# A two-layer hybrid block on one core: the recurrence as three streams in a TensorE order written by the program, and attention scores over the full array

## The chip, the cores and the metric

The kernel runs on one core of one Trainium2 chip. The metric is the device time of one execution, in microseconds; smaller is better. TensorE does the matrix products, VectorE (DVE), ScalarE (ACT) and GpSimd (POOL) the element-wise work, SyncE (SP) issues most transfers. Each engine executes its own list of instructions strictly in the order in which they stand in the built program.

## What is computed

Two layers act on 512 latent tokens and 256 context tokens of width 2048. Each layer normalises and modulates its input, multiplies it with one wide matrix (7872 columns), and feeds four groups of heads: a spatial-gating MLP, differential attention, a recurrence in two directions, and a short convolution. Each group is gated, the four are joined, and one output product follows. The change touches the recurrence, the attention scores and the convolution:

```python
def rwkv_scan(r, k, v, decay, kk, a, s0):
    def step(S, inp):
        r_t, k_t, v_t, w_t, kk_t, a_t = inp
        sa = jnp.einsum('bhvk,bhk->bhv', S, -kk_t)
        S = (S * w_t[:, :, None, :] + sa[..., None] * (kk_t * a_t)[:, :, None, :]
             + v_t[..., None] * k_t[:, :, None, :])
        y = jnp.einsum('bhvk,bhk->bhv', S, r_t)
        return S, y
...
def diff_attn_core(q, k, v, lam):
    s = _f32(jnp.einsum('bqhmd,bkhmd->bhmqk', q, k)) * (HD_QK ** -0.5)
    p = jax.nn.softmax(s, axis=-1)
    a = p[:, :, 0] - lam * p[:, :, 1]
```

## The kernel before

**Main passes.** Every column tile of the wide product (`mtile`, `mstep`) is computed transposed: 128 output columns by 512 latent tokens in one PSUM bank and by 256 context tokens in another. Weights and activations are each split into a high and a low part, and three products are summed (high by high, high by low, low by high), over 16 blocks of 128 rows. So a tile is 48 passes of 512 columns and, where the context is needed, 48 of 256. They all stand on line 306 and are called main passes here. The split of the weights (lines 276 and 277) is done by ACT and by POOL or DVE.

**The recurrence.** The 768 tokens are cut into three segments of 256 and each segment into four chunks of 64. Per layer there are four feature tiles by three segments by two directions: 24 segment rounds. A round has these parts:

- `seg_pre` and `seg_scores` prepare a segment. On TensorE: `lw`, `la` (lines 603 to 605), the squared norm `n` (line 684, called from line 631), the bonus sum `bs` (line 684, called from line 665), a transposition `vp`, the scores `g` (line 706) and a transposition `bt`. From `n` to `bs` there is a long way over other engines: square root on ACT (632), maximum, reciprocal and product on DVE (633, 634, 636), the products `bk` on POOL (652, 656), `BK` on DVE (658), the product `t_L` on DVE (661) and on POOL (663), and its split `hi`, `lo` (276, 277). `t_L` is written in place of a tile that `BK` reads, so line 661 stands behind line 658.
- `seg_inverse` inverts a triangular matrix by doubling: some 14 groups of products in f16 and fp32 (lines 804, 809, 848), each of which needs the group before it, after a copy on ACT or a product on DVE.
- `seg_chain` carries the state through four chunks: per chunk three products in a row, lines 745, 748 and 753, each after a copy or an update on DVE and ACT.
- `seg_y` makes the output, and after both directions of a feature tile `rwkv_merge` normalises it (lines 870 and 876).

`rwkv_pipe` emits these parts in rounds: the chain of segment n, the inverse of n+1, the preparation of n+2. Main passes of the projections are emitted between rounds. The final order on every engine, TensorE too, is made by the framework's scheduler, which moves main passes in between the products.

**Attention.** Per head and per block of 128 queries, `attention` computes the scores with a product over 128 rows (line 997, query high and low parts stacked by key high part) and a second one over 64 rows only (line 999, query high part by key low part `klo`), each over 256 and 512 keys.

Of the kernel before, what the change touches and what calls it, by code (L numbers as in the profile page):

```python
# [9 lines left out]
F32 = mybir.dt.float32  # L10
# [50 lines left out]

def shape_constants():
# [38 lines left out]
    return c, h, cs, rot  # L101


class Kernel:
# [188 lines left out]
    def mstep(self, grp, w, raw, q, first, last):  # L293

        nc = self.nc
# [12 lines left out]

    def mtile(self, w_ap, w, ctx, lat, q0=0, acc=None, pre=None):
        grp = self.mopen(w, ctx, lat, acc)  # L310
        for iq in range(4):
            q = (q0 + iq) % 4
            raw = pre[iq] if pre and iq < len(pre) else self.wload(w_ap, w, q)
            self.mstep(grp, w, raw, q, iq == 0, iq == 3)
# [5 lines left out]
    def proj(self, l, c0, ctx=True, acc=None):  # L320
        ahead = self.ahead.pop(c0, None)
        if ahead:
            if ctx and ahead[1][0] is None:
                return self.mtile(self.w_cols(l, c0), W_TILE_AT[c0], self.hc, None)[0], ahead[0][0]
            return ahead[1][0], ahead[0][0]
        return self.mtile(self.w_cols(l, c0), W_TILE_AT[c0], self.hc if ctx else None, self.hl, 0, acc)
# [104 lines left out]
    def recurrence(self, l):  # L431
        nc, tc, ps = self.nc, self.tc, self.ps
        need = l < DEPTH - 1
        with tc.tile_pool(name=self.nm("rw"), bufs=1, reuse_waits="tile") as rp:
# [12 lines left out]
            def gate_tiles(fts):  # L447
                for ft in fts:
                    p = self.proj(l, 5312 + ft * 128, ctx=need)
                    t = self.gate2(rp, p, "stg", 2)  # L450
                    lo = 0 if need else NCTX
                    nc.sync.dma_start(out=self.gd[ft][:, lo:T], in_=t[:, lo:T])

            def rkv_tile(ft, i, acc=None):
                p = self.proj(l, 3584 + i * 512 + ft * 128, ctx=(need or i > 0), acc=acc)
# [5 lines left out]
            if not need:  # L461
                gate_tiles(range(3))
                for ft in range(2):
                    rkv_tile(ft, 0, ((ps, "ps", 2), (ps, "ps", 2)))
                gate_tiles((3,))
                for ft in range(2, 4):
                    rkv_tile(ft, 0)
            for d in range(2):
# [3 lines left out]
                self.evac(raw[0:96, 2:258], raw[0:96, 260:772], self.proj(l, 5120 + 96 * d), 96)  # L472
# [16 lines left out]
            late = []  # L489
            for ft in range(4):  # L490
                for i in range(0 if need or ft >= 4 else 1, 3):
                    if ft:
                        late.append((6 * ft - 2 - 1, rkv_tile, (ft, i)))
                    else:
                        rkv_tile(ft, i)
                if need or ft >= 4:
                    late.append((6 * ft + 6 - 4, gate_tiles, ((ft,),)))
            late.sort(key=lambda x: x[0])
            for n in self.rwkv_pipe(l):
                while late and late[0][0] <= n + 1:  # L500
                    _, fn, args = late.pop(0)
                    fn(*args)
            for f in range((2, 4)[l]):
                self.conv(l, f)

    def rwkv_pipe(self, l):
# [7 lines left out]
        merge = None  # L514
        for n in range(-2, N + 1):
            gens = []
            if 0 <= n < N:
                gens.append((self.seg_chain(segs[n]), 5))
            if 0 <= n + 1 < N:
                gens.append((self.seg_inverse(segs[n + 1]), 8))  # L520
            if n + 2 < N:
                gens.append((self.seg_pre(segs[n + 2]), 4))
            if merge is not None:
                gens.append((merge, 3))
                merge = None
            prog = [0.0] * len(gens)
            live = set(range(len(gens)))
            while live:
                g = min(live, key=lambda x: (prog[x], x))
                try:  # L530
                    next(gens[g][0])
                    prog[g] += 1.0 / gens[g][1]
                except StopIteration:
                    live.discard(g)
            if 0 <= n < N:
                self.seg_y(segs[n])
                if segs[n]["last"]:
                    merge = self.rwkv_merge(l, segs[n]["ft"], segs[n]["st"]["yacc"], segs[n]["st"]["bacc"])
            if n + 2 < N:
                self.seg_scores(segs[n + 2])  # L540
            yield n

    def seg_pre(self, s):
# [55 lines left out]
        yield  # L599

        lw = ps.tile([128, 512], F32, tag="ps", name=self.nm("lw"))
        la = ps.tile([128, 512], F32, tag="ps", name=self.nm("la"))
        nc.tensor.matmul(out=lw[:, 0:SEG], lhsT=wh[:, 0, d, :], rhs=lz[:, 0, :], start=True, stop=False)
        nc.tensor.matmul(out=lw[:, 0:SEG], lhsT=wlo[:, d, :], rhs=lz[:, 0, :], start=False, stop=True)
        nc.tensor.matmul(out=la[:, 0:SEG], lhsT=wh[0:96, 1, d, :], rhs=lz[0:96, 1, :], start=True, stop=True)
        tw, ta = tmp("tw"), tmp("ta")
        A.activation(out=tw, in_=lw[:, 0:SEG], func=AF.Tanh, scale=0.5, bias=col(der["w0"], q))
        A.activation(out=ta, in_=la[:, 0:SEG], func=AF.Tanh, scale=0.5, bias=col(der["a0"], q))
# [20 lines left out]
        A.activation(out=sq, in_=z["k"], func=AF.Square, scale=col(der["kk"], q))  # L629
        n2 = ps.tile([128, 512], F32, tag="ps", name=self.nm("n2"))  # L630
# [6 lines left out]
        yield  # L637
# [21 lines left out]
        if want_y:  # L659
# [3 lines left out]
            G.tensor_tensor(out=rk, in0=rk, in1=ta, op=ALU.mult)  # L663
            bs = ps.tile([128, 512], F32, tag="ps", name=self.nm("bs"))
# [21 lines left out]
    def seg_scores(self, s):  # L686
        l, d, want_y, AR, BK, zv = (s[k] for k in ("l", "d", "want_y", "AR", "BK", "zv"))
        nc, rp, ps = self.nc, self.rp, self.ps
        V, G, A = nc.vector, nc.gpsimd, nc.scalar
        vp = ps.tile([128, 4, 128], F32, tag="ps", name=self.nm("vp"))  # L690
# [12 lines left out]
        for c2 in range(0, 4, 2):  # L703
            g = ps.tile([128, 2, 2, nk, 64], F32, tag="ps", name=self.nm("g"))
            for c in range(2):
                nc.tensor.matmul(out=g[:, c], lhsT=bkc(c2 + c), rhs=AR[:, c2 + c, :, 0:nk, :], start=True, stop=True)  # L706
            for c in range(2):
                mk = self.gmask[:, d:d + 1, 0:nk].to_broadcast([128, 2, nk, 64])
                V.tensor_tensor(out=GM[:, c2 + c, 0:nk].rearrange("p k h t -> p h k t"), in0=g[:, c], in1=mk,
                                op=ALU.mult)  # L710
        bt = ps.tile([128, 4, 128], F32, tag="ps", name=self.nm("bt"))
# [4 lines left out]
    def seg_chain(self, s):  # L716
# [5 lines left out]
        hs2 = (slice(0, 64), slice(64, 128))  # L722
        two = lambda t: t.rearrange("p a t -> p (a t)")
# [3 lines left out]
        for n in range(4):  # L727
# [18 lines left out]
            V.tensor_copy(out=zs[0:64], in_=chp[0:64, 0:64])  # L746
            A.copy(out=zs[64:128], in_=chp[64:128, 64:128])  # L747
            nc.tensor.matmul(out=chp[:, 128:192], lhsT=XT32[:, c, :], rhs=zs, start=True, stop=True)  # L748
            V.tensor_copy(out=UV[0:64, c, 0, :], in_=chp[0:64, 128:192])
            A.copy(out=UV[64:128, c, 1, :], in_=chp[64:128, 128:192])  # L750
            if end:
                break
            nc.tensor.matmul(out=chp[:, 192:320], lhsT=BKT[:, c, :], rhs=two(UV[:, c]), start=True, stop=True)  # L753
            if n == 3:
                S = rp.tile([128, 64], F32, tag=f"S{d}", bufs=2, name=self.nm("S"))
            for h, hs in enumerate(hs2):
                src = chp[hs, 192 + 64 * h:256 + 64 * h]
                dst = S[hs] if n == 3 else SV[hs, cn, h, :]
                if sp is None:
                    V.tensor_scalar(out=dst, in0=src, scalar1=pc[hs], scalar2=None, op0=ALU.mult)  # L760
                else:
                    V.scalar_tensor_tensor(out=dst, in0=src, scalar=pc[hs], in1=sp[hs], op0=ALU.mult, op1=ALU.add)  # L762
            yield
        st["S", d] = S

    def seg_y(self, s):
# [4 lines left out]
        if want_y:  # L771
            yp = ps.tile([128, 4, 2, 64], F32, tag="ps", name=self.nm("yp"))
            two = lambda t: t.rearrange("p a t -> p (a t)")
            for c in range(4):
                nc.tensor.matmul(out=yp[:, c], lhsT=two(UV[:, c]), rhs=GM[:, c, 1], start=True, stop=False)
                nc.tensor.matmul(out=yp[:, c], lhsT=two(SV[:, c]), rhs=AR[:, c, :, 1, :], start=False, stop=True)
            if "yacc" not in st:
                st["yacc"] = rp.tile([128, PADW], F32, tag=("o", "yacc")[ft % 2], name=self.nm("yacc"))
# [9 lines left out]
    def seg_inverse(self, s):  # L788
# [31 lines left out]
        xs = lambda h, hs, c: XT[hs, c, 64 * h:64 * h + 64]  # L820
        mm2(aX, XT, lambda c: self.eyeh, part(lambda c: c == 0, no))
        mm1(aXT, lambda h, hs, c: self.eyeh[hs], xs, part(no, no))
        X = t16("X", 2)
        A.copy(out=X, in_=aX)
        for j in range(1, 6):
            p1 = pst()
            mm2(p1, ET, lambda c: X[:, c, :])
            T1 = t16("T1")
            V.tensor_tensor(out=T1, in0=p1, in1=bt(self.lm(d, j)), op=ALU.mult)  # L829
# [3 lines left out]
            if j < 5:  # L833
                Xn = t16("X", 2)
                A.copy(out=Xn, in_=aX)  # L835
                X = Xn
            XT = XTs[j % 2]
            for h, hs in enumerate(hs2):
                A.copy(out=half(XT, h), in_=aXT[hs])  # L839
            yield  # L840
        wide = lambda: ps.tile([128, 4, 128], F32, tag="iv", bufs=1, name=self.nm("inv"))
        p = wide()
        mm2(p, XT, lambda c: self.eyef)
        X32 = rp.tile([128, 4, 128], F32, tag="X32", name=self.nm("X32"))
        A.copy(out=X32, in_=p)
# [3 lines left out]
        yield  # L849
        for h, hs in enumerate(hs2):  # L850
            V.tensor_tensor(out=half(Rb, h), in0=half(p, h), in1=half(X32, h), op=ALU.subtract)
# [11 lines left out]
    def rwkv_merge(self, l, ft, y, bacc):  # L863
# [3 lines left out]
        for seg in range(0 if need_ctx else 1, 3):  # L867
            s = slice(seg * SEG, (seg + 1) * SEG)
            mp = ps.tile([128, 512], F32, tag="ps", name=self.nm("mp"))
# [4 lines left out]
            A.activation(out=sq, in_=y[:, s], func=AF.Square)  # L874
            vp = ps.tile([128, 512], F32, tag="ps", name=self.nm("vp"))
# [417 lines left out]
```

## Time and profile before

| | us |
|---|---|
| three runs: median (lowest to highest) | 3799.59 (3787.55 to 3809.05) |
| the profiled execution: its time | 3795.03 |
| its span in the trace | 3793.2 |
| TensorE busy in it | 3508.6 (92%) |
| DVE, ACT, POOL busy | 2300.1, 1866.6, 1338.5 |
| mean granted share of TensorE's clock | 0.956 |

The profiled execution lies within the three runs, and the argument is made against its time. A busy TensorE is one that has some product in flight; since products overlap, busy time says little about how close it is to its full rate, and the distance between the starts of consecutive products says more. First layer's recurrence: about 218 to 968 us; second layer's: 2313 to 3016 us. Attention and the gating MLP follow each.

### The profile page before, as it was taken

The page shows a single profiled execution, that of the slowest core. Times are in us where ns is not written, and L with a number is a line of the kernel's source. Part 1 is how long each engine was busy: PE and PEld are TensorE (multiplying, and loading weights), DVE is VectorE, ACT ScalarE, POOL GpSimd, SP SyncE. Part 2 cuts the span into 40 slices and gives each one's busy share as a digit, 9 for nine tenths or more (in the row PEclk, how much of TensorE's full clock was granted, in tenths as well). Part 3 has the DMA queues.
Part 4 walks back from the last instruction along what each step waited for, and adds up shares of the span by engine and source line. Part 5 has one row for each costly group of instructions (what it writes and reads, how often), then busy time and mean ns, then how long its engine had stood idle before and what let it go on. Part 6 is the DMA issues. An engine that isn't in the chain of part 4 may idle for free. (4 is left out here: it accounts for less than half of the span.)

```text
span 3793.2 us, 61920 instructions
## 1 busy us (share of the span) xinstructions
PE 3508.6 (92%) x22388; PEld 2829.0 (75%) x22388; DVE 2300.1 (61%) x4659; ACT 1866.6 (49%) x4131; POOL 1338.5 (35%) x1713
## 2 busy tenths in 40 slices
PE   6999999989999999999897899999778999999998
PEld 1477777767877877888776777777566787777797
DVE  5856777776376536463778734767667526643355
ACT  3466676765234344223324435767666524444454
POOL 2244444544222212222444433445334332222243
PEclk9999999989999999999999999999668999999999
DMA  8432222211343313343655433122011244422565
GB/s 299 181 114 66 58 65 67 62 44 44 104 120 95 98 57 95 109 139 119 201 158 184 124 110 93 55 66 63 27 29 45 64 148 129 123 62 81 158 194 180
DMA packets 239746, 400.89 MB, mean 106 GB/s; under 512 B 25936, under 2 KB 95568, under 8 KB 235344
## 3 DMA queue, kind: packets, MB, share of 16 engines
q1 hardware_dynamic: 232528, 386.45, 33.7%
q10 hardware_dynamic: 6912, 10.49, 0.8%
q8 instruction: 176, 2.88, 0.3%
q14 instruction: 130, 1.06, 0.1%
HBM read 363.28 MB, written 33.56 MB: 105 GB/s over the span
## 5 line engine op out<-in xcount | busy, mean ns | idle before, releaser
L306 PE MATMUL p<-h,wh 128*128 128x512 f32 (+3 forms) x8576 | 2175.9, 351 | 35.9 <-ACT y L1160 10.6
L306 PEld LDWEIGHTS p<-h,wh 128*128 128x128 f32 (+1 forms) x8576 | 1419.7, 191 | 250.6 <-issue 17.8
L306 PE MATMUL p<-h,wl 128*128 128x512 f32 (+2 forms) x4288 | 1350.8, 351 | 39.7 <-DVE wl L277 26.1
L277 POOL TENSOR_TENSOR wl<-wr,wh 128x512 fp32r<-128x512 f32 (+1 forms) x535 | 761.8, 1426 | 1606.5 <-ACT wh L276 1441.6
L276 ACT CAST wh<-wr 128x512 fp32r<-128x512 f32 (+1 forms) x756 | 466.5, 618 | 1001.0 <-PE p L306 792.3
L306 PEld LDWEIGHTS p<-h,wl 128*128 128x128 f32 (+1 forms) x4288 | 751.5, 191 | 143.2 <-DVE wl L277 32.8
L222 DVE SCALAR_TENSOR_TENSOR acc<-gw,sil,acc 128x512 f32<-128x512 f32 (+1 forms) x636 | 449.3, 763 | 33.4 <-DMA gw<-in_w_mod 31.2
L277 DVE TENSOR_TENSOR wl<-wr,wh 128x512 fp32r<-128x512 f32 (+1 forms) x221 | 160.6, 727 | 223.7 <-ACT wh L276 222.1
L804 PEld LDWEIGHTS <-ib 128*128 128x128 f16 x2304 | 133.7, 104 | 138.2 <-issue 70.9
L839 ACT CAST ib<-xa 64x256 f16<-64x256 f32 x480 | 176.4, 368 | 17.5 <-PE xa L809 11.7
L1001 DVE TENSOR_REDUCE sm<-s 128x1 f32<-128x256 f32 (+1 forms) x144 | 76.5, 542 | 102.0 <-PE s L999 99.5
L829 DVE TENSOR_TENSOR T<-inv,c 128x256 f16<-128x256 f32 x240 | 99.1, 413 | 37.0 <-PE inv L804 33.9
L741 POOL TENSOR_SCALAR sp<-SV,pcs 64x64 f32<-64x64 f32 x160 | 80.9, 510 | 108.1 <-DVE SV L762 83.4
L745 PE MATMUL ch<-SV,GM 128*128 128x128 f32 x384 | 90.0, 319 | 17.2 <-DVE SV L762 9.8
L652 POOL TENSOR_TENSOR bk<-t_tw,kr 64x256 f32<-64x256 f32 x96 | 92.7, 966 | 36.8 <-DVE kr L636 33.1
L1008 ACT ACTIVATE e<-s,sm 128x256 f32<-128x256 f32 (+1 forms) x144 | 80.9, 568 | 48.8 <-DVE sm L1005 39.4
L706 PE MATMUL g<-AR,BK 128*128 128x256 f32 (+1 forms) x384 | 96.0, 389 | 3.8 <-DVE BK L658 2.0
L748 PE MATMUL ch<-zs,xb 128*128 128x64 f32 x384 | 81.5, 297 | 15.2 <-ACT zs L747 13.8
L753 PE MATMUL ch<-UV,BKT 128*128 128x128 f32 x352 | 85.5, 328 | 10.2 <-ACT UV L750 9.2
L748 PEld LDWEIGHTS ch<-zs,xb 128*128 128x128 f32 x384 | 65.7, 204 | 38.8 <-ACT zs L747 32.7
L762 DVE SCALAR_TENSOR_TENSOR SV<-ch,pcs,sp 64x64 f32<-64x64 f32 x256 | 72.0, 281 | 36.7 <-PE ch L753 29.0
L835 ACT CAST X<-xa 128x256 f16<-128x256 f32 x192 | 71.4, 372 | 45.5 <-PE xa L809 43.0
(269 smaller groups left out, 5018.9 us busy)
## 6 DMA issues: line engine op xcount, KB each, us to landing
wr<-in_w_in SPq DMA_DIRECT2D x484, 256.0 KB, 2.7
wr<-in_w_out SPq DMA_DIRECT2D x256, 256.0 KB, 2.9
gw<-in_w_mod SPq DMA_DIRECT2D x192, 256.0 KB, 3.0
gw<-in_w_mod SPq DMA_DIRECT2D x32, 1024.0 KB, 6.7
gw<-in_w_mod SPq DMA_DIRECT2D x128, 128.0 KB, 3.1
raw<-rkvd SPq DMA_DIRECT2D x96, 128.5 KB, 2.1
lz<-lzd SPq DMA_DIRECT2D x48, 256.0 KB, 3.1
os<-od SPq DMA_DIRECT2D x32, 256.0 KB, 3.3
```

The costliest lines, as they stand in the source:

```text
L222: self.nc.vector.scalar_tensor_tensor(out=acc, in0=w, scalar=s, in1=acc, op0=ALU.mult, op1=ALU.add)
L276: self.nc.scalar.copy(out=hi, in_=raw)
L277: eng.tensor_tensor(out=lo, in0=raw, in1=hi, op=ALU.subtract)
L306: nc.tensor.matmul(out=p[0:w, 0:n], lhsT=a[:, kk, :], rhs=x[b][k], start=(first and kk == 0 and i == 0), stop=(last and kk == 3 and i == 2))
L652: G.tensor_tensor(out=bk[hs, :, h, :], in0=c4(an)[hs], in1=kn[hs], op=ALU.mult)
L706: nc.tensor.matmul(out=g[:, c], lhsT=bkc(c2 + c), rhs=AR[:, c2 + c, :, 0:nk, :], start=True, stop=True)
L745: nc.tensor.matmul(out=chp[:, 0:128], lhsT=two(GM[:, c, 0]), rhs=two(SV[:, c]), start=True, stop=True)
L748: nc.tensor.matmul(out=chp[:, 128:192], lhsT=XT32[:, c, :], rhs=zs, start=True, stop=True)
L753: nc.tensor.matmul(out=chp[:, 192:320], lhsT=BKT[:, c, :], rhs=two(UV[:, c]), start=True, stop=True)
L804: nc.tensor.matmul(out=out[:, c, :], lhsT=lhsT[:, c, :], rhs=rhs(c), **kw(c))
L829: V.tensor_tensor(out=T1, in0=p1, in1=bt(self.lm(d, j)), op=ALU.mult)
L839: A.copy(out=half(XT, h), in_=aXT[hs])
```

## The change

Three things are changed.

1. **TensorE's order inside the recurrence is written by the program.** The generators of the recurrence now yield before each dependent product, with an assumed cost on TensorE and an assumed delay from the product before it (`CHAIN_LAT` and `INV_LAT`, 1.3 us, for the chain and the inverse; 3.0 and 4.0 us for the two steps from `n` to `bs`). A function `interleave` runs four streams: chains with outputs, inverses, preparations with merges, and the main passes of a list of tiles. It keeps its own clock: at each point it picks the first of the three recurrence streams whose assumed delay has passed, or else the next main pass; and a main pass also when the recurrence is ahead of its share. The order so found is fixed for TensorE (`manual_schedule`); the other engines are still ordered by the scheduler, where the copies of chain and inverse now have high priority.
2. **The low part of the attention keys is laid out over 128 rows** (`klo[m]`, with a copy on POOL), so that line 999's product runs over the full array like line 997's. It adds the product of the two low parts.
3. **Buffers.** All outputs of the recurrence use one tile `yacc`, `la` shares the bank of `lw`, and the convolution's input and output share one tile.

```diff
+CHAIN_LAT = 1.3
+INV_LAT = 1.3
...
+                new = first and kk == 0 and i == 0 and grp[1][0] is not None
+                yield sum(n for p, _, n in grp if p is not None) / 2220.0, 1.2 if new else 0.0
...
+            with tc.manual_schedule(engines={nc.tensor.engine}):
+                self.interleave(l, jobs, first)
...
+        def chains():
+            for m, s in enumerate(segs):
+                yield 0.0, 0.0, False, [("inv", m, 2.0)]
+                yield from self.seg_chain(s)
+                if m % 6 == 0 and m:
+                    yield 0.0, 0.0, False, [("merge", m // 6 - 1, 0.0)]
+                yield from self.seg_y(s)
+                mark(("y", m))
...
+        strs = [chains(), inverses(), scores(), mains()]
...
+        while any(r is not None for r in req):
+            t = [ready(i) if req[i] is not None else None for i in range(4)]
+            pick = next((i for i in range(3) if t[i] is not None and t[i] <= now), None)
+            if t[3] is not None and t[3] <= now:
...
+                ahead = start is not None and sum(used[0:3]) / total_r > (used[3] - start) / (total_m - start)
+                if pick is None or (ahead and req[pick][0] > 0):
+                    pick = 3
+            if pick is None:
+                now = min(x for x in t if x is not None)
+                continue
+            cost, _, bank, _ = req[pick]
+            now += cost
...
+        yield 0.23, 1.5, True
         n2 = ps.tile([128, 512], F32, tag="ps", name=self.nm("n2"))
         self.head_sums(n2, sq)
...
-        yield
+        yield 0.0, 3.0, False
...
             G.tensor_tensor(out=rk, in0=rk, in1=ta, op=ALU.mult)
+            yield 0.23, 4.0, True
             bs = ps.tile([128, 512], F32, tag="ps", name=self.nm("bs"))
             self.head_sums(bs, rk)
...
+            yield 0.43, CHAIN_LAT, False
             chp = ps.tile([128, 320], F32, tag="ch", bufs=1, name=self.nm("ch"))
...
+            with hp():
+                V.tensor_copy(out=zs[0:64], in_=chp[0:64, 0:64])
+                A.copy(out=zs[64:128], in_=chp[64:128, 64:128])
...
-                klo = tT("klo", dt=F32R)
+                klo = [tT(f"klo{m}", dt=F32R) for m in range(2)]
...
+                    G.tensor_copy(out=klo[m][b, cs], in_=klo[m][a, cs])
...
-                    nc.tensor.matmul(out=s_[:, 0:n], lhsT=qk["q"][m][ms, qs], rhs=klo[ms, ks],
+                    nc.tensor.matmul(out=s_[:, 0:n], lhsT=qk["q"][m][:, qs], rhs=klo[m][:, ks],
```

Three places in TensorE's order follow. The first is in the first layer's recurrence, in one segment each: the squared norm `n` (line 684 before, 778 after) and the bonus sum `bs` of that segment. `p` rows are main passes (line 306 before, 324 after), `ch` rows the chain, `inv` and `xa` rows the inverse. Before:

```order
L684 MATMUL n_708_3679<-hi_3680,bonesr 128x256
L753 MATMUL ch_3527<-UV_3519,BKT_2674 128x128
L684 MATMUL n_708_3679<-lo_3681,bonesr 128x256
...
L684 MATMUL bs_3757<-hi_3758,bonesr 128x256
L306 MATMUL p_5168<-h_967,wh_5231 128x256
L306 MATMUL p_5167<-h_959,wl_5232 128x512
L684 MATMUL bs_3757<-lo_3759,bonesr 128x256
L306 MATMUL p_5168<-h_966,wl_5232 128x256
```

and after:

```order
L778 MATMUL n_797_4234<-hi_4235,bonesr 128x256
L778 MATMUL n_797_4234<-lo_4236,bonesr 128x256
L324 MATMUL p_4064<-h_717,wl_4214 128x512
L324 MATMUL p_4065<-h_724,wl_4214 128x256
...
L911 MATMUL inv_4348<-X_4333,ib_1308 128x64
L778 MATMUL bs_4355<-hi_4356,bonesr 128x256
L778 MATMUL bs_4355<-lo_4357,bonesr 128x256
L324 MATMUL p_4064<-h_959,wh_4311 128x512
```

Between `n` and `bs` stood 48 main passes, 7 products of the chain, 28 products of line 804 and 32 of line 809; now there are 26 main passes, 4 products of the chain, 16 and 16. `bs` has moved closer to `n`.

The second place is in the second layer's recurrence, a stretch between two products of one chunk. Before, without a main pass near it (the rows from line 745 over line 748 to line 753):

```order
L745 MATMUL ch_29680<-SV_29076,GM_29079 128x128
L706 MATMUL g_29404<-AR_22685,BK_29322 128x256
...
L706 MATMUL g_29409<-AR_22685,BK_29322 128x256 x2
L748 MATMUL ch_29680<-zs_29681,xb_22692 128x64
L713 MATMUL bt_29414<-cst,BK_29322 128x128 x4
L603 MATMUL lw_29814<-lz_29733,wlh_27905 128x256
...
L753 MATMUL ch_29680<-UV_29672,BKT_29080 128x128
```

and the same kind of stretch after (line 849, formerly 748, then 856, formerly 753, then 844, formerly 745):

```order
L849 MATMUL ch_30175<-zs_30176,xb_22678 128x64
L324 MATMUL p_30115<-h_21006,wh_30203 128x512
...
L324 MATMUL p_30115<-h_21005,wl_30204 128x512
L324 MATMUL p_30115<-h_21012,wh_30203 128x512
L324 MATMUL p_30115<-h_21013,wh_30203 128x512
L856 MATMUL ch_30175<-UV_30149,BKT_29643 128x128
L324 MATMUL p_30115<-h_21012,wl_30204 128x512
...
L844 MATMUL ch_30262<-SV_29639,GM_29642 128x128
```

Main passes have moved in between the chain's products.

The third place is the end of the second layer's recurrence, where the last merge (lines 870 and 876, now 989 and 996) is followed by the main passes of the attention. Before:

```order
L306 MATMUL p_32827<-h_21025,wh_32848 128x512
L306 MATMUL p_32827<-h_21026,wh_32848 128x512
L876 MATMUL vp_32197<-gn_32195,cst 128x256
L306 MATMUL p_32827<-h_21025,wl_32849 128x512
L306 MATMUL p_32827<-h_21032,wh_32848 128x512
```

and after:

```order
L856 MATMUL ch_33330<-UV_33308,BKT_33058 128x128
L844 MATMUL ch_33344<-SV_33054,GM_33057 128x128
L849 MATMUL ch_33344<-zs_33345,xb_22679 128x64
L856 MATMUL ch_33344<-UV_33308,BKT_33058 128x128
...
L989 MATMUL mp_33389<-yacc_32725,cst 128x256
L996 MATMUL vp_33394<-gn_33392,cst 128x256
L324 MATMUL p_33707<-h_20977,wh_33711 128x512
```

Main passes that stood among the last merge's products now stand behind all of it, and the last rounds have none among them.

## Rows read from the trace of the kernel before

**Rows 1.** Busy time by stretch: start:end, length, then engines; recurrences of both layers.

```profile
217.70:967.90 750.20, 706.91 (x5791) 573.52 (x5790) 539.89 (x1229) 493.92 (x1233) 337.52 (x600) 0.97 0.21 59
2312.70:3015.70 703.00, 612.16 (x4860) 482.99 (x4859) 490.19 (x1163) 471.11 (x1173) 303.31 (x562) 0.88 0.18 50
```

**Rows 2.** Timeline of TensorE: start, us, engine, line, shapes; three short pieces.

```profile
199.92 0.28 PE L306 MATMUL p<-h,wl 128*128 128x256 f32 x1
200.04 0.40 PE L306 MATMUL p<-h,wh 128*128 128x256 f32 x2
...
504.41 0.39 PE L775 MATMUL yp<-GM,UV 128*128 128x128 f32 x2
504.63 0.39 PE L776 MATMUL yp<-AR,SV 128*128 128x128 f32 x2
...
2215.53 0.39 PE L306 MATMUL p<-h,wl 128*128 128x512 f32 x1
2215.76 0.61 PE L306 MATMUL p<-h,wh 128*128 128x512 f32 x2
```

**Rows 3.** Line 306 by stretch: length, PE and PEld busy, granted clock, DMA.

```profile
2650.00:2700.00 50.00, 0.00 (x0) 0.00 (x0) 0.67 0.07 19
...
2850.00:2900.00 50.00, 14.82 (x44) 7.50 (x44) 0.80 0.12 34
```

**Rows 4.** Waits of TensorE's weight loads in 217.7 to 967.9: total, times, longest.

```profile
PEld bs L684 <- ACT hi L276: 12.5, 15, 3.4
```

**Rows 5.** Timeline of 598 to 612 us, all engines: from `n` to `bs`.

```profile
598.42 0.39 PE L684 MATMUL n<-lo,bonesr 128*128 128x256 f32 x1
...
602.44 1.75 DVE L634 RECIPROCAL t_sq<-t_sq 128x256 f32<-128x256 f32 x1
...
605.61 1.87 POOL L652 TENSOR_TENSOR bk<-t_tw,kr 64x256 f32<-64x256 f32 x2 [0.38 <-DVE kr L636]
...
610.33 0.73 POOL L663 TENSOR_TENSOR t_L<-t_L,t_ta 128x256 f32<-128x256 f32 x1 [1.15 <-DVE t_L L661]
...
611.55 0.39 PE L684 MATMUL bs<-hi,bonesr 128*128 128x256 f32 x1 [0.39 <-ACT hi L276]
```

**Rows 6.** Timeline of TensorE in the stretch without main passes, second layer.

```profile
2718.59 0.36 PE L684 MATMUL n<-lo,bonesr 128*128 128x256 f32 x1
...
2732.12 0.58 PE L684 MATMUL bs<-hi,bonesr 128*128 128x256 f32 x1
...
2743.21 0.38 PE L684 MATMUL n<-lo,bonesr 128*128 128x256 f32 x1 [0.25 <-DVE lo L277]
```

**Rows 7.** Attention scores: line 997 in all, then TensorE's timeline.

```profile
L997 PE MATMUL s<-k,q x144: 274/387/628, 1086.2 to 3444.4; 128*128 128x256 f32 x80, 128*128 128x512 f32 x64
...
1201.77 0.27 PE L997 MATMUL s<-k,q 128*128 128x256 f32 x1
1201.98 0.38 PE L999 MATMUL s<-klo,q 64*128 64x256 f32 x1
1202.29 0.38 PE L306 MATMUL p<-h,wl 128*128 128x256 f32 x1
...
1204.51 0.40 PE L997 MATMUL s<-k,q 128*128 128x512 f32 x1
1204.84 0.50 PE L999 MATMUL s<-klo,q 64*128 64x512 f32 x1
1205.27 0.71 PE L1029 MATMUL op<-aT,vt 128*128 128x128 f32 x4
```

**Rows 8.** Timeline of TensorE after a gap, first passes of the second layer.

```profile
2207.41 0.73 PE L306 MATMUL p<-h,wh 128*128 128x512 f32 x2 [3.42 <-ACT wh L276]
...
2210.54 0.63 PE L306 MATMUL p<-h,wl 128*128 128x512 f32 x1
2210.97 0.63 PE L306 MATMUL p<-h,wh 128*128 128x512 f32 x1
```

**Rows 9.** Busy time in the first layer's attention, columns as in the first group.

```profile
1032.80:1540.00 507.20, 494.50 (x2696) 403.64 (x2695) 299.62 (x573) 196.54 (x414) 113.80 (x77) 0.99 0.31 93
```

More of the change, by code (lines that the diff above doesn't have):

```diff
@@ L59, with run @@
 NCST = _n
+def run(gen):
+    while True:
+        try:
+            next(gen)
+        except StopIteration as e:
+            return e.value
 def shape_constants():
@@ L293, in mstep, with g_mstep @@
     def mstep(self, grp, w, raw, q, first, last):
+        run(self.g_mstep(grp, w, raw, q, first, last))
+    def g_mstep(self, grp, w, raw, q, first, last):
         nc = self.nc
@@ L459, in rkv_tile, with lora_tile @@
                 nc.sync.dma_start(out=self.rkvd[ft][i][:, lo:T], in_=t[:, lo:T])
[L461 to L468, printed above, removed]
+            def lora_tile(d):
                 raw = rp.tile([128, PADW], F32, tag="x", name=self.nm("lraw"))
@@ L513, in rwkv_pipe @@
         N = len(segs)
[L514 to L541, printed above, removed]
+        done, now = {}, 0.0
@@ new lines, in merges, with scores @@
+        def merges(ft):
+            st = segs[6 * ft]["st"]
+            yield 0.0, 0.0, False, [("y", 6 * ft + 5, 1.0), ("gate", ft, 4.0)]
+            yield from self.rwkv_merge(l, ft, st["yacc"], st["bacc"])
+            mark(("merge", ft))
+        def scores():
+            for m, s in enumerate(segs):
+                if m % 6 == 0:
+                    yield 0.0, 0.0, False, [("lora", 1, 6.0)] + [("rkv", m // 6, i, 4.0) for i in range(3)]
+                if m > 2:
+                    yield 0.0, 0.0, False, [("y", m - 3, 0.0)]
+                yield from self.seg_pre(s)
+                if m > 1:
+                    yield 0.0, 0.0, False, [("y", m - 2, 0.0)]
+                yield from self.seg_scores(s)
+                mark(("scores", m))
+                if m % 6 == 1 and m > 6:
+                    yield from merges(m // 6 - 1)
+            yield from merges(3)
@@ new lines, in mains, with advance @@
+        def mains():
+            for key, gen in jobs:
+                yield from gen
+                mark(key)
+        if l == DEPTH - 1:
+            for key in (("gate", 0), ("gate", 1), ("gate", 2), ("rkv", 0, 0), ("rkv", 1, 0)):
+                mark(key)
+        strs = [chains(), inverses(), scores(), mains()]
+        req, last, used, banks = [None] * 4, [0.0] * 4, [0.0] * 4, [0.0, 0.0]
+        def advance(i):
+            try:
+                r = next(strs[i])
+                req[i] = (tuple(r) + (False, []))[:4] if len(r) == 2 else (tuple(r) + ([],))[:4]
+            except StopIteration:
+                req[i] = None
@@ new lines, in ready @@
+        def ready(i):
+            cost, lat, bank, keys = req[i]
+            t = last[i] + lat
+            if bank:
+                t = max(t, min(banks))
+            for k in keys:
+                if k[:-1] not in done:
+                    return None
+                t = max(t, done[k[:-1]] + k[-1])
+            return t
+        for i in range(4):
+            advance(i)
+        start, total_m, total_r = None, self.main_us(l) - 30.0, N * (15.1, 14.1)[l]
+        while any(r is not None for r in req):
+            t = [ready(i) if req[i] is not None else None for i in range(4)]
+            pick = next((i for i in range(3) if t[i] is not None and t[i] <= now), None)
+            if t[3] is not None and t[3] <= now:
+                if start is None and all(k[:-1] in done for k in [("lora", 1, 0)] + [("rkv", 0, i, 0) for i in range(3)]):
+                    start = used[3]
+                ahead = start is not None and sum(used[0:3]) / total_r > (used[3] - start) / (total_m - start)
[6 more added lines that the diff above has]
+            now += cost
+            last[pick] = now
+            used[pick] += cost
+            if bank:
+                banks.remove(min(banks))
+                banks.append(now + 1.4)
+            advance(pick)
@@ L1101, in conv @@
             G.memset(zp[:, c:c + 2], 0.0)
[L1102 removed]
+        p = (yield from self.g_proj(l, 6848 + f * 128, ctx=ctx))
         for i, o0, n, po in segs:
```

163 lines of the change are left out of this document (99 added, 64 removed).

## The prediction

> **What bounds the kernel now.** I began with busy time by stretch [rows 1]. In the first layer's recurrence TensorE is busy 707 of 750 us, in the second layer's 612 of 703, with DVE at 72% and 70% and ACT below: TensorE leads, but is it working or waiting? So I read its timeline for the distance between starts [rows 2]. A main pass of 512 columns takes 0.23 us, one of 256 columns 0.12, an fp32 product of 128 columns (two records) 0.22. Pricing every product so, in the order as built, from the first `lw` to the last merge product, gives TensorE 608 us of work in the first layer (1747 main passes, 304 us; the recurrence's own products 304) and 477 us in the second (977 passes, 193; own products 284). The rest of the two spans, 142 and 226 us, is waiting: some 6 us in each of the first layer's 24 rounds. Third, the main passes by stretch [rows 3]: from 2650 to 2850 us, four rows alike, the second layer has none, because the order had used them up (the next are at 2850); the granted clock stands at 0.67 there and rounds still take 24.6 us (from one `n` to the next, 2718.59 to 2743.21 [rows 6]). There the bound is the delay of dependent products, not TensorE. In attention TensorE is busy 494.5 of 507.2 us [rows 9].
>
> So there are three places to gain: short waits at many links, the starved stretch, and what attention costs TensorE.
>
> **The change part by part.** *Main passes moved into the recurrence.* In the new order the same span holds 2112 passes in the first layer and 1596 in the second: 673 and 617 us of work, 65 and 140 more. That work leaves places where TensorE ran without waits (ahead of and behind the recurrence), so by itself it changes nothing. The stage lengths to beat are therefore 750 + 65 = 815 us and 703 + 140 = 843 us.
>
> *Waits at the links.* I counted the work that stands between each product and the one that needs it. In the first layer before, 25, 35 and 56 of some 90 links behind lines 745, 748 and 753 had less than 1.25 us of it, and 244 of 335 links of the inverse; after, 19, 18, 16 and 60. Copies also move ahead on DVE and ACT. About half a microsecond a round goes to switches into the 64x64 products and stays. I take the 6 us of a round down to 3. Bounds: 1 (switches and a little) and 6 (nothing gained, since DVE and ACT are as busy as before).
>
> *A new wait at `bs`.* `bs` needs a walk over ACT, DVE, POOL, DVE, POOL and ACT. In the timeline the second product of `n` starts at 598.42, the reciprocal at 602.44, `bk` at 605.61, the product on POOL at 610.33, and `bs` at 611.55: 13.1 us [rows 5]. Where no main pass competes it is 2718.59 to 2732.12, 13.5 us [rows 6]. Now TensorE waited for it 15 times in 24, 12.5 us in all [rows 4], because 11.3 us of work stood in between (median, first layer). The new order leaves 6.5 us: the program assumed 3.0 + 4.0. What stands behind `bs` in TensorE's list are main passes and the next products of chain and inverse, and all wait with it. How long will the walk be? Bare durations on it add to about 8.4 us, hops aside; as it runs today it is 13.1 to 13.5. DVE's list from the maximum to line 661 holds a little less than before (7.1 us of instructions against 7.8, by the durations in the trace). I take the middle, 11 us. Less 6.5 of work and 0.8 of the link waits that fall into this window anyway, 3.7 us remain. 34 of the 40 `bs` have so little cover (22 and 12; the others stand in the tails): 126 us. Bounds: 34 x (8.9 - 7.3) = 54 and 34 x (13.1 - 7.3) = 197.
>
> *Tails.* The new order has used up its passes before the end: two rounds without any in the first layer (14 us of work with the merge), four in the second (38 us), and the attention's passes now stand behind the last merge. A round with all parts but no passes takes 24.6 us [rows 6]; one with the chain alone I put at 19, between 12 links of 1.2 and that row. First layer: 2 x 19 + 14 for the merge = 52, idle 38. Second: 2 x 24.6 + 2 x 19 + 14 = 101, idle 63.
>
> *Sum of the recurrences.* Outside the tails there are 22 and 20 rounds. First layer: 673, + 22 x 3 = 66, + 22 x 3.7 = 81, + 38, is 858 against 815: 43 us lost. Second: 617, + 20 x 3 = 60, + 12 x 3.7 = 44, + 63, is 784 against 843: 59 us won. The starved stretch is filled, and the wait at `bs` eats most of it.
>
> *Attention.* Two score products over 512 keys take 1204.51 to 1205.27, 0.76 us, over 256 keys 1201.77 to 1202.29, 0.52 us [rows 7]; two main passes of the same columns take 0.46 and 0.24 [rows 2]. There are 64 and 80 pairs [rows 7]: 64 x 0.30 + 80 x 0.28 = 42 us, all on TensorE, which bounds that stage [rows 9]. Bound below: 20, if the softmax between the pairs takes half back. The 16 added copies on POOL lie beside main passes (POOL is busy 114 of 507 us); uncovered, about 1.4 us once a head, 11 us. The Trainium skill speaks against this edit: "TensorEngine Tiling (Array Packing)", Performance Considerations, recommends row tiling where the contraction is 64 or less, for up to twice the speed. By that rule the 64-row product should be the cheap one and the edit lose some 12 us (half of the two widths, 144 times). The trace disagrees: the 64-row product takes 0.43 us to its successor where a full-array pass takes 0.23.
>
> *The rest at nothing:* one `yacc` makes an output wait for the merge six rounds earlier, which the chain of the next round (over 20 us) covers; the convolution's shared tile delays one evacuation by the output's transfer, a few us twice.
>
> Sum: the profiled execution's 3795 + 43 - 59 - 42 = 3737 us; the three runs' median is 4.6 us above that execution, so half of the difference is added: **3740**.
>
> **The rivals.** *The wait at `bs` doesn't come.* If TensorE runs late enough elsewhere, or the walk shrinks to 7 or 8 us, 126 us fall away: 3614. For it: the reciprocal waited 4 us behind other work in rows 5. Against: even alone the walk took 13.5.
>
> *The walk stays at 13.1 us or more* (slower). Then each of 34 waits is 5.8 us: 71 us more, 3811; it decides from about 13 us on. There may be a second price: after the idle gap of 3.42 us at 2207.41, passes take 0.43 us (2210.54 to 2210.97), which is the lower of the two clock levels [rows 8]; some 4 us at that level after every long wait, half of them lost, would add up to 65 us, 3876. "TensorE: Matmul & The Clock Gate", Part 1, in the Trainium skill, states that idling lowers the clock; the rows agree.
>
> *The links gain nothing.* DVE and ACT queues, not the cover, make the waits; 6 us a round stay: 42 x 3 = 126 us more, 3866. For it: DVE is over 70% busy, and links with cover had waits too.
>
> *Attention gains nothing* (the rule above, or the softmax bounds the stage): 3782 to 3794.
>
> **How the numbers follow.** Forecast (3700 to 3780): 0.46. No wait at `bs`: 0.22. Walk of 13 us: 0.15. Links gain nothing: 0.12. Attention nothing: 0.05. A change under 0.5% (19 us) can't be told from none in this kernel. Faster takes nearly all of the first two: 0.66. Same takes the attention case and the edges of the forecast and of the slower cases: 0.15. Slower takes the rest: 0.19. The range reaches from below the second case to between the slower ones, 3600 to 3835; outside remain some 0.06 and 0.13. The forecast's own range is 3700 to 3780.
>
> **What will show it.** Waits of TensorE at `bs` for the split on ACT: near 3.7 us each, 34 times (right), or below 1 (first rival), or above 5 (second). Spans from first `lw` to last merge product near 858 and 784 us. Passes in every 50 us of the second layer, and the clock near 1.0 up to the tail. Score products 0.23 and 0.12 us apart. I am wrong if the first layer's recurrence gets shorter than 815 us, or the second's isn't shorter than 843.

## The result and the profile after

The changed kernel takes 4010.62 us (median of 4 runs, 4004.77 to 4013.26) beside 3795.94 us of the kernel before: ratio 1.056, 95% interval 1.0526 to 1.0594. It is slower by 215 us, where 3740 us and a gain were forecast, and it lies outside the range. Run once more beside the last experiments it took 4009.31 us, ratio 1.0592 (1.0574 to 1.0611).

The profiled execution's span grew from 3793.2 to 4008.0 us. Busy time of the changed kernel's two recurrences, columns as in [rows 1]:

```profile
224.00:1172.80 948.80, 800.48 (x6154) 666.91 (x6152) 548.49 (x1243) 508.59 (x1251) 351.76 (x611) 0.91 0.18 51
2464.80:3344.20 879.40, 734.49 (x5478) 585.86 (x5476) 512.40 (x1188) 501.32 (x1225) 356.91 (x603) 0.90 0.20 57
```

They took 750 and 703 us before [rows 1]: 199 and 176 us more. The passes that moved in shorten the stretches where they stood by 173 us: behind the last merge product 65 and 95 us become 10 and 10, and what lies between the two layers' stages loses 33. The first layer's attention, from its first `rot` to the first `mx`, takes 587 us instead of 556; the second layer's 329 instead of 357. The recurrence starts 6 us later, and the gating stage of the first layer takes 4 more. That is 199 + 176 - 173 + 31 - 28 + 6 + 4 = 215.

What TensorE waits for in the whole changed kernel (engine, its product and line, releaser; total us, times, longest):

```profile
PE bs L778 <- ACT hi L289: 121.3, 38, 7.1
PE p L324 <- ACT x L356: 39.8, 9, 10.1
PE ch L856 <- ACT UV L852: 35.9, 43, 2.6
PE ch L849 <- ACT zs L847: 26.8, 38, 2.3
PE p L324 <- DVE wl L290: 24.6, 18, 4.3
PE n L778 <- ACT hi L289: 17.5, 5, 4.6
PE vp L996 <- ACT gn L993: 17.4, 9, 3.8
PE ch L844 <- DVE SV L866: 16.8, 26, 2.2
```

The same view of the kernel before has for `bs` and for the chain's three links:

```profile
PE ch L748 <- ACT zs L747: 13.8, 26, 1.5
PE bs L684 <- ACT hi L276: 13.5, 15, 3.1
...
PE ch L745 <- DVE SV L762: 9.8, 18, 1.8
PE ch L753 <- ACT UV L750: 9.2, 23, 0.7
```

The stop at `bs` is the largest row now. But the three `ch` rows, the chain's links, have grown too. The inverse's links have not: all waits of its products in the two recurrences together fall from 60 us (26 of them in the stretch that had no passes) to 25, while those of the chain's products rise from 40 (21 there) to 83. One stop at `bs` in the timeline of all engines, beside [rows 5]:

```profile
597.91 0.28 PE L778 MATMUL n<-lo,bonesr 128*128 128x256 f32 x1
...
605.77 0.47 DVE L729 SCALAR_TENSOR_TENSOR kr<-t_zk,kkh,t_sq 128x256 f32<-128x256 f32 x1
...
606.33 2.35 POOL L745 TENSOR_TENSOR bk<-t_tw,kr 64x256 f32<-64x256 f32 x2 [3.78 <-DVE kr L729]
...
610.09 0.73 POOL L756 TENSOR_TENSOR t_L<-t_L,t_ta 128x256 f32<-128x256 f32 x1 [1.42 <-DVE t_L L754]
610.85 0.41 ACT L289 CAST hi<-t_L 128x256 fp32r<-128x256 f32 x1 [0.34 <-POOL t_L L756]
...
611.31 0.58 PE L778 MATMUL bs<-hi,bonesr 128*128 128x256 f32 x1 [5.60 <-ACT hi L289]
```

From 605.7 to 611.3 TensorE has nothing that it may start, though main passes stand right behind `bs` in its list. Busy time around this stop (start:end, length, engines, granted clock):

```profile
590.00:607.00 17.00, 14.99 (x129) 11.93 (x127) 10.40 (x24) 9.19 (x24) 8.19 (x13) 1.00 0.18 55
607.60:617.80 10.20, 6.49 (x33) 5.38 (x34) 5.92 (x13) 3.59 (x9) 3.22 (x8) 0.51 0.29 79
618.00:640.00 22.00, 21.77 (x172) 18.81 (x170) 9.21 (x27) 10.55 (x27) 7.81 (x13) 1.00 0.09 25
```

The granted clock is 0.51 from 607.6 to 617.8, in the later part of the stop and for six more microseconds of work: the lower level, 1.2 GHz. In all, the clock stands there for 176 and 183 us of the two recurrences, against 41 and 174 before. The Trainium skill, "TensorE: Matmul & The Clock Gate", Part 1, says that idling lowers the clock; the row agrees.

### The profile page after: what moved, and what is told of

The parts are those of the page before. It is cut to its first block, busy times and chain, and to the rows that moved or that the text cites. A ratio compares the mean times of both kernels' runs of the same rounds, so it can differ in the third digit from the quotient of the medians.

```text
span 4008.0 us, 61782 instructions
## 1 busy us (share of the span) xinstructions
PE 3497.2 (87%) x22388; PEld 2862.4 (71%) x22388; DVE 2297.7 (57%) x4659; ACT 1866.1 (47%) x4129; POOL 1352.1 (34%) x1729
## 5 line engine op out<-in xcount | busy, mean ns | idle before, releaser
L324 PE MATMUL p<-h,wh 128*128 128x512 f32 (+3 forms) x8576 | 2211.1, 357 | 84.1 <-ACT x L356 39.8
L324 PE MATMUL p<-h,wl 128*128 128x512 f32 (+2 forms) x4288 | 1356.2, 357 | 39.3 <-DVE wl L290 24.6
L290 POOL TENSOR_TENSOR wl<-wr,wh 128x512 fp32r<-128x512 f32 (+1 forms) x535 | 752.9, 1409 | 1569.6 <-ACT wh L289 1422.0
L235 DVE SCALAR_TENSOR_TENSOR acc<-gw,sil,acc 128x512 f32<-128x512 f32 (+1 forms) x636 | 455.6, 773 | 14.1 <-DMA gw<-in_w_mod 10.6
L778 PE MATMUL bs<-hi,bonesr 128*128 128x256 f32 x40 | 19.2, 480 | 121.3 <-ACT hi L289 121.3
L851 DVE COPY UV<-ch 64x64 f32<-64x64 f32 x192 | 40.5, 211 | 114.5 <-PE ch L849 111.7
L856 PEld LDWEIGHTS ch<-UV,BKT 128*128 128x128 f32 x352 | 63.5, 215 | 59.5 <-ACT UV L852 50.6
L949 ACT CAST X<-xa 128x256 f16<-128x256 f32 x192 | 71.5, 372 | 74.0 <-PE xa L916 71.6
```

Of the source, the lines that this page charges most:

```text
L235: self.nc.vector.scalar_tensor_tensor(out=acc, in0=w, scalar=s, in1=acc, op0=ALU.mult, op1=ALU.add)
L290: eng.tensor_tensor(out=lo, in0=raw, in1=hi, op=ALU.subtract)
```

## The experiments

The kernel before took 3782.6 to 3786.1 us beside these runs. Ratios are to it, with 95% intervals; differences in us are to the changed kernel's 4009.3 where nothing else is said.

| kernel | median us | ratio |
|---|---|---|
| `bs` later | 3879.0 | 1.0246 (1.0225 to 1.0266) |
| convolution's own tile | 3949.9 | 1.0436 (1.0418 to 1.0454) |
| before + attention edit | 3741.5 | 0.9884 (0.9866 to 0.9901) |
| passes ahead of `bs` | 3976.4 | 1.0506 (1.0484 to 1.0527) |
| order left to the scheduler | 3750.0 | 0.9904 (0.9889 to 0.9919) |
| `bs` later, latencies 1.8 | 3975.6 | 1.0500 (1.0484 to 1.0516) |
| `bs` later, tile, third convolution | 3783.5 | 0.9993 (0.9984 to 1.0003) |
| `bs` later, no priority | 4008.6 | 1.0591 (1.0573 to 1.0608) |
| scheduler's order, no priority | 3793.8 | 1.0026 (1.0011 to 1.0041) |
| scheduler's order, tile, third convolution | 3672.1 | 0.9702 (0.9684 to 0.9720) |

Two measures are worked out from the traces. A round runs here from one segment's `n` to the next one's, the last to the end of the recurrence. Its **surplus** is its length less TensorE's work in it, the work priced with distances as in [rows 2]; means over the rounds that have 40 passes or more, without the last. At a chain link the **cover** is the work that stands between a product and the one that needs it, and the **copy** is the time from the product's start to the end of its later copy; about 512 links each, with the 10th and 90th percentile.

| kernel | surplus, layers 1 and 2 | cover | copy | correlation |
|---|---|---|---|---|
| before | 6.8, 6.8 | 0.54, 2.77 | 0.91, 2.96 | 0.68 |
| changed | 11.5, 10.3 | 0.46, 1.62 | 0.77, 2.34 | 0.20 |
| `bs` later | 8.0, 7.8 | 0.41, 1.62 | 0.77, 2.47 | 0.19 |
| `bs` later, no priority | 10.1, 10.6 | 0.35, 1.62 | 0.77, 3.16 | 0.20 |
| scheduler's order | 5.9, 6.2 | 0.71, 2.41 | 0.80, 2.50 | 0.69 |
| the same, no priority | 6.9, 7.0 | 0.69, 2.85 | 0.79, 3.26 | 0.85 |

**The stop at `bs`.**

```diff
-            yield 0.23, 4.0, True
+            yield 0.23, 10.0, True
             bs = ps.tile(...)
```

> One edit to the changed kernel: the program assumes 10 us instead of 4 between the head sums n and the head sums bs, so that some 13 us of TensorE work stand between them instead of 7. In the trace of the changed kernel the walk from n to bs takes 12.5 us, TensorE stands 3.0 us (first layer, 24 times) and 3.5 us (second, 16 times) ahead of bs, 128 us in all, and most of these stops are followed by 3.4 or 6.8 us at the lower clock. Theory A (the stop at bs and the clock it lowers are what the recurrence lost): 128 us and some 30 to 60 more come back, 3820 to 3855 us. Rival B (the links of chain and inverse wait for DVE and ACT queues, and the wait moves to the next product that needs the same engines): less than 60 us come back, 3950 us or more.

130 us come back: between the theories, nearer to A. At `bs` 2.2 us of waits are left. The chain's rows take part of it over:

```profile
PE ch L856 <- ACT UV L852: 49.4, 58, 3.3
...
PE ch L849 <- ACT zs L847: 32.0, 48, 1.9
```

So A holds for the stop, and B for what is left behind it: surpluses of 8.0 and 7.8 us a round, above the 6.8 of before.

**The clock that a stop lowers.**

```diff
+            for j in range(12):
+                nc.tensor.matmul(out=bs, lhsT=self.bonesr, rhs=self.hl[0][j], start=True, stop=True)
             self.head_sums(bs, rk)
```

> The changed kernel with 12 needless 512-column passes (2.8 us) in TensorE's order ahead of each bs, into the tile that bs then overwrites: the wait stays, but TensorE works through most of it. It adds 480 passes, 111 us of work, which fit into the 128 us of waits. Theory A (each stop at bs also lowers the clock for some microseconds behind it): some 60 us less than the changed kernel, 3930 to 3970. Rival B (the lower clock behind the stops costs nothing that counts, since the links wait anyway): 4005 to 4035 us, the overshoot where a wait was shorter than 2.8 us.

33 us less, just short of A's span; the intervals of the changed kernel and of this one overlap at their ends (1.0526 and 1.0527), against the repeated run they are apart. Waits at `bs` fall from 121.3 to 32.8 us, and the time at the lower clock in the recurrences from 359 to 221 us. TensorE spends 111 us on needless passes and still waits 33, so 144 where it had waited 121, and yet the kernel is shorter by 33: the clock gives back some 56 us. That is an estimate from these rows. A second one, from the clock's records, is 46 us: the work that starts at the lower level in the recurrences, priced as above and without the needless passes, falls from 119 to 73 us.

**The order of TensorE's list.**

```diff
-            with tc.manual_schedule(engines={nc.tensor.engine}):
-                self.interleave(l, jobs, first)
+            self.interleave(l, jobs, first)
```

> The changed kernel without the fixed TensorE order: streams, latencies, copies and passes are as they are, but the scheduler that placed the instructions before places them again. By its order 11.6 us (first layer) and 13.6 us (second) of TensorE work stand between n and bs, against 7.2 and 7.2 in the fixed order. Theory A (the fixed order with its assumed 4 us is what makes the stop at bs): the stop goes as in the run with 10 us, and the ratio to the kernel before is 1.02 to 1.03, about 3880 us. Rival B (the loss lies in the streams and tiles themselves): 1.045 to 1.06, 3955 us or more.

Better than both: 259 us less than the changed kernel, and 1% faster than the kernel before. With the same streams, tiles and priorities, the recurrences take 804 and 771 us. The waits of the chain and of `bs` in this run, beside those of the changed kernel:

```profile
PE ch L848 <- ACT zs L846: 12.3, 27, 1.0
...
PE ch L855 <- ACT UV L851: 9.5, 17, 1.7
...
PE ch L843 <- DVE SV L865: 7.2, 14, 1.3
...
PE bs L777 <- ACT hi L289: 6.9, 12, 3.3
```

The second table says what differs. Copies end about as late in both orders, but the written order puts nearly the same work, 0.46 to 1.62 us, behind every link, since it assumes 1.3 us for each; the scheduler puts more where the copy comes later (correlation 0.69 against 0.20), as it did in the kernel before (0.68). That is not all: against the run with the later `bs` the recurrences are 128 us shorter, some 76 of it in the rounds with passes and 53 in the rounds at the end, for which the scheduler's order kept more passes (72 in the first layer's last round, not 9).

**Copies and their priority.**

```diff
-        hp = self.tc.high_priority
+        hp = contextlib.nullcontext
```

On top of the later `bs`, and then on top of the scheduler's order:

> The kernel with 10 us ahead of bs, with the raised priority of the copies behind the products of chain and inverse taken away, so that DVE and ACT take them in the old order. Theory A (the links wait for those engines' queues, and the priority shortens that: from product to finished copy on ACT a median of 1.6 us before and 1.0 to 1.4 after): waits behind chain and inverse rise by 2 us a round or more, 50 to 100 us in all, 3930 to 3980. Rival B (the cover in TensorE's order decides and the priority does little): within 20 us of 3879.

> TensorE's order left to the scheduler, and the raised priority of the copies behind the products of chain and inverse taken away. In the fixed order that cost 130 us. Theory A (the fixed order is dear because its cover between two links is nearly the same everywhere, 0.5 to 1.6 us, while ACT's and DVE's copies take 0.8 to 2.4; the scheduler puts more work where the copy comes later): the order follows the later copies, and it costs less than half, 3770 to 3815 us. Rival B (the order matters only through bs, the priority acts by itself): 130 us again, 3870 to 3890.

In the written order it costs 130 us, theory A's cause but above its 50 to 100; in the scheduler's 44, as theory A had it. So ACT's and DVE's queues do decide when a link is ready, and the order that doesn't follow them pays three times as much for it. The lower clock has a part in this: of the 2.1 and 2.8 us by which the written order's rounds get longer, some 0.9 is work that starts at the lower level.

**A larger constant.**

```diff
-CHAIN_LAT = 1.3
-INV_LAT = 1.3
+CHAIN_LAT = 1.8
+INV_LAT = 1.8
```

> On top of the 10 us ahead of bs, the program assumes 1.8 us instead of 1.3 between two links of the chain and of the inverse. The work between the links rises from a median of 1.6 us to 1.9, but the passes are used up some five rounds (first layer) and six rounds (second) before the end. Theory A (links wait because ACT's copy is done up to 2.4 us behind the product, later than the program assumes): in rounds that have passes TensorE's time beyond its work falls from about 8 us to 5 or 6; the starved rounds at the end cost more than that wins, in all 0 to 80 us more than with 10 us alone (3880 to 3960). Rival B (the 8 us of a round are switches and the lower clock, not late copies): rounds with passes keep their 8 us, and the starved rounds add 100 us or more (3980).

97 us more than with the later `bs` alone, close to B's figure: rounds with passes have surpluses of 7.6 and 6.7 us, a little less than 8.0 and 7.8 but not A's 5 or 6, and the starved rounds at the end cost more. A larger constant covers the late copies a little better and uses up the passes by rounds too early.

**Tail and tile.**

```diff
-        x = gp.tile([...], F32, tag="o", ...)
+        x = gp.tile([...], F32, tag="o" if gp is self.rp else "x", ...)
```

> One edit to the changed kernel: behind the attention heads the convolution's first product is evacuated into the tile x again, as before, instead of the tile o that the head's output still occupies. Theory A (the shared tile costs the first layer's attention stage its 31 us: TensorE waits there 5 times for that evacuation, 31.5 us): 3975 to 3985 us. Rival B (the 31 us come from the wider score products or from POOL's copies): within 8 us of the changed kernel, 4003 or more.

59 us less, more than theory A's 24 to 34 and than the waits named: the first layer's attention takes 533 us, 580 in the repeated run of the changed kernel, and the rest is spread thin. What happens without the edit is seen in the changed kernel's timelines of SP's queue, ACT and TensorE, one piece each:

```profile
1408.22 0.33 SPq L1164 DMA_DIRECT2D od<-o  x1
```

```profile
1411.61 0.37 ACT L356 COPY x<-p 128x256 f32<-128x256 f32 x1 [8.88 <-DMA od<-o]
```

```profile
1412.03 0.80 PE L324 MATMUL p<-h,wh 128*128 128x256 f32 x2 [10.07 <-ACT x L356]
```

The evacuation waits until the attention head is finished and its output has left the tile, and TensorE waits 10 us for the accumulator.

```diff
-        n = (23.3, 34)[l]
+        n = (27.3, 34)[l]
...
-                jobs += [gate(1)] + [rkv(3, i) for i in range(3)] + [gate(2), conv(1), gate(3)]
+                jobs += [gate(1)] + [rkv(3, i) for i in range(3)] + [gate(2), conv(1), conv(2), gate(3)]
...
-            late = ({('a', 1): 2, ('a', 3): 3}, {})[l]
+            late = ({('a', 3): 3}, {})[l]
```

> On top of the 10 us ahead of bs and of the convolution's own tile behind the attention heads, the third convolution of the first layer (357 passes, 61 us of work) moves from behind an attention head into the recurrence, where it stands in the last round, in which TensorE had 24.6 us of work in 80.7 us. Theory A (the tail without passes idles, and work put there is free): the own tile gives some 45 us and the tail another 45, against the kernel with 10 us alone: about 3790 us, ratio 1.00. Rival B (the last chain and merge wait behind the passes, so that the tail only gets longer): the own tile's 45 us alone, 3830 to 3850.

Theory A: 95 us less than with the later `bs` alone, from both edits together. The last round now holds 71.6 us of work in 85.6 us, where 24.6 stood in 80.7: 47 us of work for 5.

**Attention alone.** The edits to `klo`, its copy on POOL and the two score products, put into the kernel before.

> The kernel before with the attention edit alone (low parts of k in both halves of the array, copied by POOL; score products over 128 rows). The prediction's term: 42 us less, 3753 us. What the second layer's attention showed in the changed kernel, 28 us less for 80 pairs, with the same for 64 pairs, gives 22 more: about 3745. Rival (the softmax between the pairs bounds that stage, or the wider product costs more): 3782 to 3800 us.

41 us less, and the two attention stages are 27 and 18 us shorter. The pairs in the changed kernel's timeline of TensorE, beside [rows 7]:

```profile
1230.23 0.28 PE L1116 MATMUL s<-k,q 128*128 128x256 f32 x1
1230.35 0.28 PE L1118 MATMUL s<-klo,q 128*128 128x256 f32 x1
1230.47 0.28 PE L1116 MATMUL s<-k,q 128*128 128x256 f32 x1
...
1246.80 0.39 PE L1116 MATMUL s<-k,q 128*128 128x512 f32 x1
1247.03 0.39 PE L1118 MATMUL s<-klo,q 128*128 128x512 f32 x1
1247.26 0.28 PE L1116 MATMUL s<-k,q 128*128 128x256 f32 x1
```

A pair takes 0.24 and 0.46 us to its successor, not 0.52 and 0.76. The Trainium skill ("TensorEngine Tiling (Array Packing)", Performance Considerations) recommends row tiling for a contraction of 64. The prediction's 12 us took the gain for a product that stands alone. No run here tests two such products side by side; in the kernel before each one stands alone among products over the full array, and that was the dear form. Its extra price hardly depends on the width: in [rows 7] about 0.1 us ahead of it (0.21 and 0.33 us, where full-array passes take 0.12 and 0.23) and 0.2 behind it (0.31 and 0.43). That speaks for a price of the change of form on either side, not of the product itself.

**Together, and the control.**

> The streams with TensorE's order left to the scheduler, the convolution's own tile behind the attention heads, and the first layer's third convolution moved into its recurrence. By the single runs: 3750 less 45 for the tile, less 15 to 25 for the last round of the first layer (31 us beyond its work in the run with the free order): 3680 to 3695 us, ratio 0.97 to 0.976, below both kernels. Rival (the tile's gain is part of the free order's): 3705 to 3735.

> The changed kernel itself, without an edit, in the same session as the last two kernels, so that they stand beside it. By its ratio of 1.053 to 1.059: 3985 to 4010 us beside a kernel before of 3786.

3672 us, 3.0% below the kernel before and 337 us below the changed one, a little better than expected. Its recurrences in busy time by stretch:

```profile
220.40:1052.10 831.70, 799.28 (x6462) 668.64 (x6460) 551.10 (x1257) 516.50 (x1271) 365.40 (x623) 1.00 0.21 63
2238.50:3009.40 770.90, 712.83 (x5478) 560.34 (x5476) 513.55 (x1188) 497.98 (x1225) 353.53 (x603) 0.95 0.22 65
```

The control repeats the result.

## Why the prediction was wrong

**The step that failed** is "I take the 6 us of a round down to 3". With the stop at `bs` removed, the written order's rounds have 8.0 and 7.8 us of surplus, where the kernel before had 6.8 and I had put 3 less. In that run the recurrences take 875 and 828 us; the prediction's terms without the stop give 777 and 740. Of these 186 us the tails make 6 (below) and the 42 rounds outside them 180, 4.3 us each: some 7 us a round instead of 3, the largest part of the 270 us between 3740 and 4010.

My evidence was that fewer links had less than 1.25 us of work behind them. That count was true, and it was the wrong one: a link waits when its own copy ends later than its own cover. In the rounds with passes of that run, chain links whose copy ends more than 0.3 us after their cover hold TensorE 1.0 us beyond the work, links whose copy ends before it 0.2. Fewer are late than in the kernel before (141 of 437, not 173 of 346), but a late one costs 1.0 us instead of 0.7, since the written order makes the cover even, not fitting. So the chain's links take 4.6 us a round where they took 4.4, and waits outside chain and inverse, at `n`, merges and main passes, grow from 0.5 to 1.2 us a round. The scheduler's order has 155 late links of 442 at 0.5 us each, and its chain links take 2.9 us a round.

The lower clock has a smaller part: work that starts at the lower level adds 0.7 and 0.8 us a round in that run, 0.3 and 0.4 in the kernel before. The rival "the links gain nothing" named DVE's and ACT's queues and was nearest in its cause (3866 forecast; the rival of the longer walk with a second price for the clock came to 3876), but held that cover doesn't help, which the scheduler's order refutes: it brings the surplus below that of before, though by 1 us, not 3.

**The stop at `bs`** came as forecast: 126 us were expected, the waits' row shows 121.3 in 38 stops, and moving `bs` gave 130. Inside that term errors cancel: the walk took 12.5 us, not 11, other waits in the same stretch covered 2.7 of it, not 0.8, and there were 38 stops, not 34. So the rivals without the stop, or with one much dearer, fall. **The lower clock** behind the stops, put into a rival as a second price, was real, at some 46 to 56 us.

**Tails** came out near the sum. Cut as the prediction cut them, from the first chain product of the first round that has no passes, two and four rounds take 53 and 107 us in the run with the later `bs`, where 52 and 101 were forecast. In the changed kernel's passes by stretch, beside [rows 3], the starved stretch has gone from the middle to the end:

```profile
3250.00:3300.00 50.00, 0.00 (x0) 0.00 (x0) 0.70 0.01 4
```

**The convolution's tile**, "a few us twice", was mis-sized: the transfer is short, but the tile comes free only when the whole attention head is done. 59 us hang on it, and it hid the attention's gain in the first layer.

**Right in size** was the attention: 42 us forecast, 41 measured alone. **The moved passes** gave back 173 us where they had stood, not the 205 that I had counted; which work took the other 32 was not tried.

Added up against the two profiled executions (215 us longer, where 58 shorter was forecast: 273 us): the rounds 180, the tails 6, the moved passes 32, the two attention stages 45, most of it the tile, and the start and the gating stage 10; the stop at `bs` came out even. The clock lies inside the rounds' and the stop's figures.

How far each cause of the scheduler's gain over the written order reaches is not settled to the last microsecond: 130 of its 259 us came back with the later `bs` alone; the rest lies at chain, inverse, merge and `n` and in the fuller rounds at the end, and the table of covers shows the chain alone. That cover which follows the copies wins in the rounds with passes is borne out by the two runs without priority. Why the scheduler's order follows the copies and keeps passes for the end is not shown by any run.

## What to carry to other kernels

An order written by the program is only as good as its latencies: one constant for links whose copies take 0.8 to 2.5 us loses against an order whose cover follows the copies, and every product behind a late one waits with it. Compare each link's cover with its own copy in the trace, not with a threshold. Price a shared tile by when its last reader is done, and keep independent work for the last round, where it was almost free.

## What the runs showed of the hardware

Short stops are dearer than they are long. Around a stop of 5.6 us the granted clock was 0.51 over 10.2 us, six of them behind the stop; the changed kernel, with 38 stops at `bs`, stands at the lower level for 138 us more than the same kernel with needless passes ahead of `bs`, which was shorter by 33 us although TensorE did 111 us more work. And a product over 64 rows between products over 128 cost 0.28 to 0.30 us more than a full-array one, whether it had 256 or 512 columns.
